# Gate and up projections of a decoder trunk as seven products of halves, two of their four weight sums added by transfers, and the down projection in three parts

## The chip, the core and the metric

One core of one Trainium2 chip runs the whole program. Engines are named as in the profile: PE (TensorE matmul), PEld (its weight load), DVE (VectorE), ACT (ScalarE), POOL (GpSimd), SP (SyncE, which here only issues transfers). The metric is the device time of one execution, in microseconds (us), from the first to the last instruction with the little that lies around them.

## The reference

Two decoder layers on x of 512 tokens by 1024 features, in float32. Each layer adds half a SwiGLU channel mixer, then a token mixer (block-sparse attention with a spatial gate in layer 0, differential attention in layer 1), then another half SwiGLU; a last RMS norm follows. There are so four channel mixers, and they hold most of the arithmetic:

```python
def swiglu(x, w_gate, w_up, w_down):          # w_gate, w_up: 1024 x 2816, w_down: 2816 x 1024
    return (jax.nn.silu(x @ w_gate) * (x @ w_up)) @ w_down
x = x + 0.5 * swiglu(rms_norm(x, ffn_pre_norm[layer]), ...)
```

## The kernel before

Features lie on the 128 partitions and tokens on the free axis, so x is 8 tiles of 128 x 512 (`x[k]`). A float32 matmul is made of three matmuls in the type fp32r: both operands are split into a high part (a copy to fp32r on ACT) and a low part (the difference, on DVE), and `mm3` (L151) adds high x high, high x low and low x high in PSUM. Weights come in raw chunks of 128 x 1024 words over SP's queue and are split in the same way: `split_to` (L83) makes `w_hi` on ACT (L89) and `w_lo` on DVE (L90).

A `Stream` (L62) holds the order of the work as slots. Each slot is a few products with the weight chunks that they take. `run` (L129) goes through the slots: it splits the chunks of this slot, issues the loads two chunks ahead, splits the next slot's chunks, traces the aftermath that earlier slots put off with `later`, and then the slot's products. Each engine takes its instructions in an order that the tile framework derives from this order of tracing and from what it reckons to be ready.

A channel mixer is `ffn` (L273). The 22 tiles of 128 of its hidden features are worked in two halves of 11. For each tile f there is a slot for gate and a slot for up: `project` (L266) runs 8 row tiles k with three matmuls of 512 columns each, 24 matmuls, into one PSUM bank. `product` (L277) then multiplies both banks by the norm's per-token factors (L279, L282), takes SiLU on ACT (L280), multiplies (L283) and splits the result (L262, L263). After 11 tiles `down` (L313) adds that half's part into each of the 8 output tiles: 11 x 3 matmuls of 512 columns per tile, in two chunks of 6 and 5 tiles, and then one DVE operation onto `x[d]` (L323). Behind the second half each finished `x[d]` is fed to the next norm: `Norm.split` (L196) makes the moving operands xh (ACT, L200) and xl (DVE, L201), and `square` (L204) adds up the squares, on POOL (L212, L214). The factors themselves come later (`only_row`, L230: two 512-column matmuls with ones and ten DVE operations).

A token mixer's last projection is `out_proj` (L340); it feeds the same norm. `Stream.begin` (L93) orders the loads and splits at the program's start.

## Time and profile before

| | |
|---|---|
| runs | 1917.41, 1915.25, 1915.66 us; median 1915.66 |
| profiled execution, first to last instruction | 1914.3 us (no other time of that execution is given) |
| instructions | 22078, of them 8692 matmuls |
| PE / DVE / ACT / POOL busy | 98% / 54% / 34% / 15% |
| DMA | 184 MB, 31% of the engines' time |
| HBM read | 174 MB, 92 GB/s |

How to read it: the span is the profiled execution's, and the median of the runs stands 1.4 us above it. A busy share is an average over stages. Matmuls overlap each other, so that a busy PE may still run below its pace: what tells is the distance from one start to the next.

### The profile page before, as it was taken

Reading aid. Unit: us, or ns where it says so; the run is one execution under the profiler, and the core shown is the slowest. Engines: PE = TensorE matmul, PEld = TensorE weight load, DVE = VectorE, ACT = ScalarE, POOL = GpSimd, SP = SyncE. Lnnn points to the kernel's source line nnn. Section 1 sums busy time; section 2 is a strip of 40 time slices with the busy share of each in tenths; the row PEclk is TensorE's granted clock in tenths of the full one; section 3 lists DMA queues with packets and bytes.
Section 4 is the critical chain, followed back from the end, with each engine's and each line's share of the span. In section 5 each row is a group of like instructions: output and inputs, shape, how many; then the busy total and the mean of one; then the engine's idle time right before and its main releaser. Section 6 shows DMA issues by size and latency. Waiting matters only on the chain.

```text
span 1914.3 us, 22078 instructions
## 1 busy us (share of the span) xinstructions
PE 1880.3 (98%) x8692; PEld 1568.1 (82%) x8692; DVE 1028.6 (54%) x1545; ACT 653.1 (34%) x993; POOL 283.8 (15%) x230
## 2 busy tenths in 40 slices
PE   8999999999999999999999999999899999999997
PEld 7888888888778888888888888888788788888886
DVE  7443444568766433444644344457788774434443
ACT  5222322334643222323332222234455432223221
POOL 0000001343440000002200000044333320000012
PEclk9999999999999999999999999999999999999998
DMA  5223332323213323333332332233233133233322
GB/s 182 99 80 107 99 99 84 125 88 100 89 56 99 99 84 105 98 92 91 106 98 84 102 110 97 79 114 110 89 89 89 36 119 98 79 110 99 99 84 82
DMA packets 58936, 184.31 MB, mean 96 GB/s; under 512 B 6848, under 2 KB 7504, under 8 KB 58832
## 3 DMA queue, kind: packets, MB, share of 16 engines
q1 hardware_dynamic: 58224, 181.82, 30.5%
q8 instruction: 68, 1.11, 0.2%
q10 hardware_dynamic: 576, 1.05, 0.1%
q14 instruction: 36, 0.29, 0.0%
q0 software_dynamic: 32, 0.03, 0.0%
HBM read 174.49 MB, written 2.10 MB: 92 GB/s over the span
## 4 chain that ended last, share of the span: by engine, by line
PE 87%; DVE 6%; POOL 3%; ACT 2%; issue 1%; DMA 0%; SPq 0%; DVEq 0%; POOLq 0%; ACTq 0%
PE py L152 10%; PE py L154 10%; PE py L153 10%; PE pu L154 8%; PE pu L152 8%; PE pu L153 8%; PE pg L153 8%; PE pg L154 8%; PE pg L152 8%; DVE w_lo L90 1%; POOL q L416 1%; PE pv L152 1%; PE pv L154 1%; PE pv L153 1%; PE pq L152 1%
## 5 line engine op out<-in xcount | busy, mean ns | idle before, releaser
L89 ACT ACTIVATE w_hi<-w_raw 128x1024 fp32r<-128x1024 f32 (+1 forms) x362 | 349.4, 966 | 958.5 <-PE py L153 323.8
L90 DVE TENSOR_TENSOR w_lo<-w_raw,w_hi 128x1024 fp32r<-128x1024 f32 (+1 forms) x362 | 414.2, 1144 | 201.9 <-ACT w_hi L89 201.3
L152 PE MATMUL pu<-xh,w_hi 128*128 128x512 f32 x736 | 286.7, 390 | 0.0
L154 PE MATMUL pu<-xh,w_lo 128*128 128x512 f32 x736 | 286.6, 389 | 0.0
L153 PE MATMUL pu<-xl,w_hi 128*128 128x512 f32 x736 | 286.6, 389 | 0.0
L152 PE MATMUL pg<-xh,w_hi 128*128 128x512 f32 x704 | 274.5, 390 | 5.1 <-ACT xh L200 5.1
L153 PE MATMUL pg<-xl,w_hi 128*128 128x512 f32 x704 | 274.6, 390 | 0.4 <-DVE xl L201 0.4
L154 PE MATMUL pg<-xh,w_lo 128*128 128x512 f32 x704 | 274.4, 390 | 0.0
L152 PE MATMUL py<-hh,w_hi 128*128 128x512 f32 x704 | 273.9, 389 | 0.0
L153 PE MATMUL py<-hl,w_hi 128*128 128x512 f32 x704 | 273.9, 389 | 0.0
L154 PE MATMUL py<-hh,w_lo 128*128 128x512 f32 x704 | 273.9, 389 | 0.0
L282 DVE TENSOR_TENSOR u<-pu,R 128x512 f32<-128x512 f32 x88 | 60.8, 691 | 267.0 <-PE pu L154 267.0
L212 POOL TENSOR_TENSOR acc<-x 128x512 f32<-128x512 f32 x6 | 9.2, 1539 | 1238.7 <-DVE x L323 1219.1
L153 PEld LDWEIGHTS pu<-xl,w_hi 128*128 128x128 f32 x736 | 138.4, 188 | 28.8
L154 PEld LDWEIGHTS pu<-xh,w_lo 128*128 128x128 f32 x736 | 138.3, 188 | 28.9
L152 PEld LDWEIGHTS pu<-xh,w_hi 128*128 128x128 f32 x736 | 138.4, 188 | 28.7
L152 PEld LDWEIGHTS pg<-xh,w_hi 128*128 128x128 f32 x704 | 132.4, 188 | 32.5 <-ACT xh L200 5.1
L153 PEld LDWEIGHTS pg<-xl,w_hi 128*128 128x128 f32 x704 | 132.4, 188 | 28.7 <-DVE xl L201 1.3
L154 PEld LDWEIGHTS pg<-xh,w_lo 128*128 128x128 f32 x704 | 132.4, 188 | 27.6
L153 PEld LDWEIGHTS py<-hl,w_hi 128*128 128x128 f32 x704 | 132.1, 188 | 27.5
L154 PEld LDWEIGHTS py<-hh,w_lo 128*128 128x128 f32 x704 | 132.1, 188 | 27.5
L152 PEld LDWEIGHTS py<-hh,w_hi 128*128 128x128 f32 x704 | 132.1, 188 | 27.3
(181 smaller groups left out, 2358.7 us busy)
## 6 DMA issues: line engine op xcount, KB each, us to landing
w_raw<-in_gu SPq DMA_DIRECT2D x174, 512.0 KB, 3.3
w_raw<-in_wd SPq DMA_DIRECT2D x64, 384.0 KB, 3.1
w_raw<-in_wd SPq DMA_DIRECT2D x64, 320.0 KB, 2.9
w_raw<-in_oqk SPq DMA_DIRECT2D x16, 512.0 KB, 3.3
ks<-ks SPq DMA_DIRECT2D x24, 256.0 KB, 3.5
w_raw<-in_eqk SPq DMA_DIRECT2D x8, 512.0 KB, 3.3
w_raw<-in_eo SPq DMA_DIRECT2D x8, 512.0 KB, 3.3
w_raw<-in_ov SPq DMA_DIRECT2D x8, 512.0 KB, 3.4
```

The lines of the kernel that those rows point to most:

```text
L89: nc.scalar.activation(hi, raw, AF.Copy)
L90: nc.vector.tensor_sub(lo, raw, hi.bitcast(F32))
L152: nc.tensor.matmul(o, sh, mh, start=first, stop=False)
L153: nc.tensor.matmul(o, sh, ml, start=False, stop=False)
L154: nc.tensor.matmul(o, sl, mh, start=False, stop=last)
L212: nc.gpsimd.tensor_mul(sq, x[k], x[k])
L282: nc.vector.tensor_mul(u, pu, norm.row)
L416: nc.gpsimd.tensor_add(q, q, sw)
```

## The change

The kernel works on pairs of hidden tiles, s and s + 11, and on gate and up of both at once. For a pair, the weights are a 2 x 2 block matrix (rows: tile s or s + 11; columns: the first or last 512 input features), a11, a12, a21, a22, each 128 x (gate, up) x 512 words. The moving side is a 2 x 2 block matrix too (first or last 512 features by first or last 256 tokens). A product of 2 x 2 blocks is made from seven block products, numbered 1 to 7 and run in the order 5, 6, 2, 7, 1 (of the next pair), 4, 3. Each is one slot of 4 row tiles x 2 (gate, up) x 3 matmuls of 256 columns, and three banks (A, B, D) collect them. Product 1 takes a11, 2 takes a12, 4 takes a22; 5 takes z = a21 + a22, 6 takes z + a11, 7 takes a21 + a11, and 3 takes a12 + (z + a11). In the first pair of each mixer all four sums are DVE additions of 1,024 words. In the others z and the operand of 7 are made by a plain load (SP) and a second load that adds onto it (`accum_op`, issued by POOL); the other two stay on DVE.

The aftermath of a pair: three ACT copies of bank A (v1, v2, v3), DVE additions and subtractions that make gate and up of both tiles from the copies and the banks, the multiplication by the factors, SiLU, the product and its split. The moving side needs seven split tiles per row tile instead of two half ones: `SevenNorm` makes them of x's halves, operands 1 and 5 when `x[0]` to `x[3]` come, the five others (`rest`) when `x[4]` to `x[7]` come. It replaces `Norm` for the four channel mixers; their factors are made as the token mixers' are (`sums`, `spread`), three slots later.

The down projection follows after pairs 0 to 3, 4 to 7 and 8 to 10. Its chunk per output tile holds both tiles of each pair, so that x gets three updates rather than two.

Slots of the channel mixers are `dense`: splits run four chunks ahead, sums one more, loads as far as six raw tiles allow. Raw chunks, halves and some mixer tiles share one pool of 14; scratch tiles go from 8 to 7 and the tiles that hold hidden features from 23 to 19.

```diff
-    BUFS = {"h": 23, "qk": 6, "tmp": 8, "row": 4}
+    BUFS = {"r2": 28, "h": 19, "tmp": 7, "row": 4}
...
+        return act.tile([P, 2, T], dt, name=name, tag="w4", bufs=14)
...
+                if dense:
+                    self.step()
+                    self.split_to(first + self.SPLIT)
+                    self.pre_to(first + self.SPLIT + 1)
+                    self.load(0, first + self.SPLIT + 8)
+                else:
+                    self.split_to(end)
+                    self.load(0, end + (2 if raws == 2 else 8))
...
+        def first(self, p):
+            self.halves(1, p, x[p][:, LO], self.gain(p))
+        def diff(self, p):
+            d = tmp("x1")[:, LO]
+            nc.vector.tensor_sub(d, x[p][:, LO], x[p][:, HI])
+            self.halves(5, p, d, self.gain(p))
+        def rest(self, p):
+            q = p + 4
+            g, n, nq = self.gain(q), neg_gains[:, self.idx, p:p + 1], neg_gains[:, self.idx, q:q + 1]
+            ta, tb = tmp("x37"), tmp("x64")
+            b22, x7, x6, x4 = ta[:, LO], ta[:, HI], tb[:, LO], tb[:, HI]
+            nc.scalar.activation(b22, x[q][:, HI], AF.Copy, scale=g)
+            nc.vector.scalar_tensor_tensor(x7, x[p][:, HI], n, b22, op0=OP.mult, op1=OP.add)
+            nc.vector.scalar_tensor_tensor(x6, x[p][:, LO], n, x7, op0=OP.mult, op1=OP.subtract)
+            self.halves(6, p, x6)
+            self.halves(2, p, x[q][:, LO], g)
+            nc.vector.scalar_tensor_tensor(x4, x[q][:, LO], nq, x6, op0=OP.mult, op1=OP.subtract)
+            self.halves(7, p, x7)
+            self.halves(4, p, x4)
+            self.halves(3, p, b22)
+        def feed(self, k):
+            if k < 4:
+                self.first(k)
+                self.diff(k)
+            else:
+                self.rest(k - 4)
+            self.square(k)
...
+    PARTS = ((0, 4), (4, 8), (8, HF))
+    ORDER = (5, 6, 2, 7, 1, 4, 3)
...
+                        if i == 0:
+                            nc.sync.dma_start(t, src)
+                        else:
+                            nc.gpsimd.dma_start(t, src, accum_op=OP.add)
...
+                if self.s > 0:
+                    by_sum = {
+                        5: lambda: Item([self.load("z", f1, 0, f1, 1)], raw("z"), frees=0),
+                        7: lambda: Item([self.load("c", f0, 0, f1, 0)], raw("c")),
+                        6: lambda: Item([], raw("z"), add("z", "z", "a11"), frees=0, free_pre=1),
+                        4: lambda: Item([self.load("a22", f1, 1)], raw("a22")),
+                    }
+                    if c in by_sum:
+                        return by_sum[c]()
+                return {
+                    1: lambda: Item([self.load("a11", f0, 0)], raw("a11"), frees=0),
+                    5: lambda: Item([self.load("a21", f1, 0), self.load("a22", f1, 1), new], raw("z"),
+                                    add("z", "a21", "a22"), frees=0),
+                    6: lambda: Item([], raw("z"), add("z", "z", "a11"), frees=0),
+                    2: lambda: Item([self.load("a12", f0, 1)], raw("a12"), frees=0),
+                    7: lambda: Item([], raw("a21"), add("a21", "a21", "a11"), free_pre=1),
+                    4: lambda: Item([], raw("a22")),
+                    3: lambda: Item([], raw("a12"), add("a12", "a12", "z"), free_pre=1),
+                }[c]()
...
+                    for p in range(4):
+                        t = norm.xt[c, p]
+                        for g in range(2):
+                            o = b[:, g * 256:(g + 1) * 256]
+                            s = slice((g * 4 + p) * P, (g * 4 + p + 1) * P)
+                            nc.tensor.matmul(o, w[0][:, s], t[:, 0], start=new and p + g == 0, stop=False, **go)
+                            nc.tensor.matmul(o, w[0][:, s], t[:, 1], start=False, stop=False, **go)
+                            nc.tensor.matmul(o, w[1][:, s], t[:, 0], start=False, stop=p == 3, **go)
...
+            def c11(self):
+                self.G = [self.both(), None]
+                nc.vector.tensor_add(self.G[0][:, :, LO], self.v_1, self.pair(self.bank["B"]))
+            def v3(self):
+                v = self.copied(-1.0)
+                self.G[1] = self.both()
+                g = self.G[1][:, :, HI]
+                nc.vector.tensor_sub(g, v, self.pair(self.bank["D"]))
+                nc.vector.tensor_mul(g, g, self.row(HI))
+            def c21(self):
+                nc.vector.scalar_tensor_tensor(self.G[1][:, :, LO], self.pair(self.bank["A"]), -1.0,
+                                               self.row(LO), op0=OP.mult, op1=OP.mult)
+                nc.scalar.activation(self.G[1][:, 0], self.G[1][:, 0], AF.Silu)
+            def c12(self):
+                g = self.G[0]
+                nc.vector.tensor_add(g[:, :, HI], self.v_2, self.pair(self.bank["D"]))
+                nc.vector.tensor_mul(g, g, self.row(slice(0, T)))
+                nc.scalar.activation(g[:, 0], g[:, 0], AF.Silu)
+            def h(self, n):
+                g = self.G[n]
+                nc.vector.tensor_mul(g[:, 1], g[:, 1], g[:, 0])
+                hi, lo = t2k("h", "hh", F32R), t2k("h", "hl", F32R)
+                nc.scalar.activation(hi, g[:, 1], AF.Copy)
+                H[self.s + n * HF] = (hi, lo)
+            def rest(self, n):
+                hi, lo = H[self.s + n * HF]
+                nc.vector.tensor_sub(lo, self.G[n][:, 1], hi.bitcast(F32))
...
+        for s0, s1 in PARTS:
+            for s in range(s0, s1):
+                for c in ORDER:
+                    if c != 1:
+                        add(s, c)
+                    elif s + 1 < HF:
+                        add(s + 1, 1)
+            cols = slice(s0 * P, s1 * P)
+            for ds in [(0, 1)] + [(d,) for d in range(2, KT)]:
+                st.add([chunk(wd[0, d][:, cols], wd[1, d][:, cols]) for d in ds], down(ds, s0, s1),
+                       dense=True, raws=6)
...
-    st.begin()
+    hi, lo = w4("w_hi", F32R), w4("w_lo", F32R)
+    for q, s in enumerate(cuts):
+        nc.scalar.activation(hi[:, :, s], a11[:, :, s], AF.Copy)
+        nc.vector.tensor_sub(lo[:, :, s], a11[:, :, s], hi[:, :, s].bitcast(F32))
+        for k in ((0,), (1,), (2, 3))[q]:
+            first.first(k)
+    st.pres = 1
+    st.halves.append([t.rearrange("p n t -> p (n t)") for t in (hi, lo)])
+    for k in range(4):
+        first.diff(k)
+    st.split_to(2)
+    for k in range(4):
+        first.rest(k)
+        if k == 1:
+            st.split_to(3)
+    for k in range(KT):
+        first.square(k, by_act=True)
     st.run()
```

## Rows read from the trace of the kernel before

**Rows 1.** The page: its span, part 1 (busy time, share of the span and instructions of each engine) and, of part 2, the granted TensorE clock in 40 slices, in tenths of full speed.

```profile
span 1914.3 us, 22078 instructions
...
PE 1880.3 (98%) x8692; PEld 1568.1 (82%) x8692; DVE 1028.6 (54%) x1545; ACT 653.1 (34%) x993; POOL 283.8 (15%) x230
...
PEclk9999999999999999999999999999999999999998
```

**Rows 2.** The page, part 4: the chain of work that ended last, its shares of the span by engine and by line.

```profile
PE 87%; DVE 6%; POOL 3%; ACT 2%; issue 1%; DMA 0%; SPq 0%; DVEq 0%; POOLq 0%; ACTq 0%
...
PE py L152 10%; PE py L154 10%; PE py L153 10%; PE pu L154 8%; PE pu L152 8%; PE pu L153 8%; PE pg L153 8%; PE pg L154 8%; PE pg L152 8%; DVE w_lo L90 1%; POOL q L416 1%; PE pv L152 1%; PE pv L154 1%; PE pv L153 1%; PE pq L152 1%
```

**Rows 3.** PE's waits over the whole span: who waited for whom, us in total, times, longest.

```profile
PE py L154 <- DVE w_lo L90: 5.3, 2, 3.1
...
PE pg L152 <- ACT xh L200: 5.1, 1, 5.1
...
PE pr L240 <- DVE lcol L184: 2.0, 1, 2.0
```

**Rows 4.** Busy time (and instructions) of each engine in four stretches: us from the span's start, length, then PE, PEld, DVE, ACT, POOL, the granted clock, the DMA engines' share and GB/s.

```profile
0.00:20.00 20.00, 14.49 (x52) 11.12 (x53) 14.07 (x26) 15.39 (x26) 2.13 (x9) 1.00 0.75 251
...
20.00:366.00 346.00, 346.00 (x1528) 286.52 (x1527) 165.13 (x197) 101.35 (x126) 21.66 (x13) 1.00 0.31 99
...
550.00:570.00 20.00, 17.76 (x78) 14.24 (x78) 19.12 (x17) 8.04 (x10) 17.57 (x11) 1.00 0.17 55
...
1520.00:1540.00 20.00, 16.90 (x74) 13.47 (x74) 19.13 (x18) 8.55 (x11) 17.63 (x12) 1.00 0.16 53
```

**Rows 5.** Timeline of a gate projection: start us, duration us, engine, line, operation. One split of a 1,024-word chunk on VectorE with GpSimd idle; the first of 24 matmuls of 512 columns, and the first of the next 24.

```profile
58.88 1.22 DVE L90 TENSOR_TENSOR w_lo<-w_raw,w_hi 128x1024 fp32r<-128x1024 f32 x1 [0.23 <-ACT w_hi L89]
...
63.21 0.39 PE L152 MATMUL pg<-xh,w_hi 128*128 128x512 f32 x1
...
68.65 0.39 PE L152 MATMUL pu<-xh,w_hi 128*128 128x512 f32 x1
```

**Rows 6.** Timeline of PE in the odd mixer's values, the first of 96 matmuls of 256 columns and the first matmul behind them; and that matmul's weight load among the groups by line and form (busy us, mean ns of one).

```profile
1312.77 0.28 PE L152 MATMUL pv<-w_hi,xh 128*128 128x256 f32 x1
...
1324.28 0.28 PE L456 MATMUL s<-ks,qs 128*128 128x256 f32 x1
...
L152 PEld LDWEIGHTS pv<-w_hi,xh 128*128 128x128 f32 x192 | 36.6, 190 | 2.6
```

**Rows 7.** The two steps of a row of factors on PE: a piece of the chain in order of time (start us, us, what), and the timeline of the end.

```profile
373.45 0.79 PE pc L223 x8
...
1904.31 1.12 PE L240 MATMUL pr<-ident,lcol 128*128 128x128 f32 x4 [2.04 <-DVE lcol L184]
```

**Rows 8.** Groups of instructions by line and form over the whole span: out<-in, tile, count, busy us, mean ns of one, idle before it.

```profile
L90 DVE TENSOR_TENSOR w_lo<-w_raw,w_hi 128x1024 fp32r<-128x1024 f32 x234 | 300.1, 1283 | 74.6 <-ACT w_hi L89 74.5
...
L89 ACT ACTIVATE w_hi<-w_raw 128x1024 fp32r<-128x1024 f32 x234 | 247.7, 1060 | 617.2 <-PE pg L153 241.3 <-issue 234.2 <-PE py L153 63.6
...
L279 DVE TENSOR_TENSOR g<-pg,R 128x512 f32<-128x512 f32 x88 | 60.8, 691 | 170.8 <-PE pg L154 170.7
...
L280 ACT ACTIVATE g<-g 128x512 f32<-128x512 f32 x88 | 54.2, 616 | 16.0 <-DVE g L279 16.0
...
L323 DVE SCALAR_TENSOR_TENSOR x<-py,x 128x512 f32<-128x512 f32 x64 | 44.3, 692 | 127.7 <-PE py L154 127.7
...
L90 DVE TENSOR_TENSOR w_lo<-w_raw,w_hi 128x768 fp32r<-128x768 f32 x64 | 61.4, 959 | 0.7 <-ACT w_hi L89 0.3
...
L201 DVE SCALAR_TENSOR_TENSOR xl<-x,gains,xh 128x512 fp32r<-128x512 f32 x48 | 64.4, 1355 | 3.3 <-ACT xh L200 3.2
```

**Rows 9.** The page, part 6: DMA issues, count, KB each, median us from issue to landing.

```profile
w_raw<-in_gu SPq DMA_DIRECT2D x174, 512.0 KB, 3.3
```

**Rows 10.** Timeline of the start.

```profile
1.33 0.71 POOL L162 DMA_DIRECT2D gains<-in_gains  x1 [0.81 <-POOLq L923]
...
3.60 0.43 DVE L108 TENSOR_TENSOR w_lo<-w_raw,w_hi 128x256 fp32r<-128x256 f32 x1 [2.36 <-ACT w_hi L107]
...
4.99 0.40 ACT L107 ACTIVATE w_hi<-w_raw 128x256 fp32r<-128x256 f32 x1
...
5.12 0.75 DVE L201 SCALAR_TENSOR_TENSOR xl<-x,gains,xh 128x512 fp32r<-128x512 f32 x1 [1.10 <-ACT xh L200]
...
5.14 0.79 PE L152 MATMUL pg<-xh,w_hi 128*128 128x512 f32 x1 [5.14 <-ACT xh L200]
...
8.59 0.68 DVE L214 TENSOR_TENSOR acc<-acc,sq 128x512 f32<-128x512 f32 x1
```

**Rows 11.** Busy time by engine (columns as in rows 4) across the first slots of the second channel mixer.

```profile
568.00:578.00 10.00, 10.00 (x46) 8.29 (x45) 9.06 (x8) 3.87 (x6) 6.06 (x4) 1.00 0.46 147
...
578.00:588.00 10.00, 10.00 (x46) 8.28 (x45) 6.08 (x10) 2.67 (x3) 0.00 (x0) 1.00 0.34 106
```

**Rows 12.** Timeline of VectorE and of GpSimd while a channel mixer's last outputs come.

```profile
901.94 1.53 DVE L201 SCALAR_TENSOR_TENSOR xl<-x,gains,xh 128x512 fp32r<-128x512 f32 x1
...
901.20 1.73 POOL L212 TENSOR_TENSOR sq<-x 128x512 f32<-128x512 f32 x1 [4.06 <-DVE x L323]
```

More of the change, by code (lines that the diff above doesn't have):

```diff
@@ L149, in trunk_kernel, with chunk, load @@
     st = Stream()
+    def chunk(*srcs):
+        keep = {}
+        def load():
+            t = w4("w_raw").rearrange("p n t -> p (n t)")
+            o = 0
+            for s in srcs:
+                nc.sync.dma_start(t[:, o:o + s.shape[1]], s)
+                o += s.shape[1]
+            keep["raw"] = t[:, :o]
+        return Item([load], lambda: keep["raw"])
     def mm3(o, sh, sl, mh, ml, first, last):
@@ L275, in ffn @@
         H = {}
-        def product(f, pg, pu):
-            g = tmp("g")
-            nc.vector.tensor_mul(g, pg, norm.row)
-            nc.scalar.activation(g, g, AF.Silu)
-            u = tmp("u")
-            nc.vector.tensor_mul(u, pu, norm.row)
-            nc.vector.tensor_mul(u, u, g)
-            H[f] = split(u, "h", "h")
-        def first(wg, wu):
-            wait = int(which == 0)
-            st.later(1 + wait, norm.only_row)
-            pg, pu = bank("pg"), bank("pu")
-            for ks in [[k] for k in range(KT)] if which == 0 else (range(KT - 1), range(KT - 1, KT)):
-                for b, w in ((pg, wg), (pu, wu)):
-                    project(b, w, norm, ks)
-            st.later(2 + wait, lambda: product(0, pg, pu))
@@ new lines, in ffn, with add, begin @@
+        steps = [Step(s, any(s == e - 1 for _, e in PARTS)) for s in range(HF)]
+        def add(s, c):
+            st.add([steps[s].item(c)], steps[s].slot(c), dense=True, raws=6)
+        add(0, 1)
+        first, end, fn, dense, raws = st.slots[-1]
+        def begin(w):
+            norm.finish_soon(3)
+            fn(w)
+        begin.tiles = steps[0].raw
+        st.slots[-1] = (first, end, begin, dense, raws)
+        for s0, s1 in PARTS:
[9 more added lines that the diff above has]
+                       dense=True, raws=6)
```

338 lines of the change are left out of this document (197 added, 141 removed).

## The prediction, made before the change was run

> **What bounds the kernel now.** I read the page first: PE is busy for 98% of the span and at the upper clock (2.4 GHz granted, 10 tenths of it) except at the very end [rows 1]. Busy PE is not proof, because matmul ends are modelled, so I read the chain of waits next: 87% of it is PE, nearly all in the gate, up and down products [rows 2]. Then PE's own list of waits: no long wait repeats, the largest is 5.3 us in two pieces at a mixer's end [rows 3]. Then the windows: through a channel mixer PE idles 0.00 us of 346 while VectorE is busy 165 us, ScalarE 101 us and the DMA engines 31% [rows 4]. So in the channel mixers (about 1,436 of 1,914 us) only PE's own pitch counts. The timeline gives it: 24 matmuls of 512 columns take 68.65 - 63.21 = 5.44 us, 0.2267 us each [rows 5].
>
> **The products.** I count by the pair of 128-wide feature tiles f and f+11; there are 44 pairs in four channel mixers. Before, a pair takes 4 projections x 24 = 96 matmuls of 512 columns: 96 x 0.2267 = 21.76 us. After, seven products x 4 row tiles x 2 (gate, up) x 3 = 168 matmuls of 256 columns. The question is whether a 256-column matmul hides its weight load. The odd mixer's values have that very shape, three matmuls with a fresh 128x128 load each: 96 of them in 1324.28 - 1312.77 = 11.51 us, 0.1199 us each, while a load shows 0.190 us and lies beside the matmul before it [rows 6]. So a pair takes 168 x 0.1199 = 20.14 us, one product 2.88 us. Saved: 44 x 1.62 = **71.1 us**; not the eighth that the count promises (2.72 per pair), because the part that does not shrink with the columns, 2 x 0.1199 - 0.2267 = 13 ns per matmul, is paid 1.75 times as often.
>
> **The row of factors.** Column sums and four transposes replace two 512-column matmuls: 0.79 + 1.12 [rows 7] - 0.45 = +1.5 us, four times; the second piece ran at the end, where the clock had fallen to 0.8, so I take **+4** (0 to 6).
>
> **Projection down in three parts.** 528 matmuls per channel mixer stay. Eight more updates of x, 0.69 us each on VectorE [rows 8], lie beside 5.44 us of PE per output tile: nothing. Without that cover they would be 5.5 us each mixer.
>
> **VectorE inside a pair.** Before: 4 splits x 1.22 [rows 5] (1.28 is the mean over the span, with GpSimd at times beside it [rows 8]) + 8 x 0.69 [rows 8] = 10.4 us of 21.76. After: 7 splits (8.5), 2 sums of 1,024 words at the price of a split (2.4), and the recombination, nine 512-wide operations and one of 1,024 (7.4): **18.4 us of 20.14**. ScalarE: 7 x 1.06 + 7 x 0.62 = 11.8 us [rows 8]. So PE still sets the pace, with 1.7 us to spare; VectorE can run near that, as it is busy 19.12 of 20 us at a mixer's end [rows 4]. Three slots of splits stand ready, and each slot's recombination comes before its split, so a delay of a slot reaches no matmul. The first pair makes all four sums on VectorE: 20.9 us, 0.8 over, in three channel mixers (the first one counts below): **+2.4** (0 to 5).
>
> **Transfers.** Two of the four weight sums of a pair move to transfers: one half is loaded by SP, the other is added by a transfer that POOL issues. Chunks per pair go from 4 to 7, 3.67 MB in 20.14 us, 182 GB/s; 99 GB/s took 31% [rows 4], so 182 take 57% by share: hidden. An adding transfer waits for the plain one (3.3 us to landing [rows 9]); behind that wait on POOL stand only the next such transfer and, in the last third, the norm's squares. The sum is split five to seven slots later, 14 to 20 us: hidden. An issue on POOL cost 0.71 us, for 28 KB in 128 rows [rows 10]; the price of one that adds 512 KB in 256 rows is not in the trace. Bounds: two a pair at 0.71 fit into VectorE's spare 1.7 even if all of it came off VectorE, which is nothing; two at twice that, 2.8, do not. I take nothing, by the row as it stands; the upper end is a rival.
>
> **The start.** VectorE must make, before the fourth product can begin: the low parts of the first chunk (1.55), four first tiles (4 x 0.43 [rows 10]), four differences (8 x 0.43), the second product's sum and split (2.44), `rest` four times (32 x 0.43 = 13.8), the third's sum and split (2.44) and the fourth's split (1.22): 26.6 us. It begins at 3.60 and so ends at 30.2; by then PE has three products, 8.6 us, and is 21.6 late. Before, 52 matmuls (11.8 us) stand in the first 20 [rows 4]: 8.2 late. **+13**; +6 if the last four operations of each `rest` are put off, +18 if the seven sums of squares (4.8 [rows 10]) come first.
>
> **From a mixer to a channel mixer, twice.** VectorE's norm tiles cost 8 x 0.75 = 6.0 before and 12 x 0.43 + 32 x 0.43 = 18.9 after; two weight sums come on top: 15.3 more. VectorE is full there already (19.12 and 19.13 of 20 us, with PE idle 2.2 and 3.1 [rows 4]) and has 0.9 + 3.9 = 4.9 us free in the following 20 [rows 11]. That leaves 10.4, of which some of the last `rest` can wait: **+9 each, 18** (3 to 15 each).
>
> **From channel mixer to channel mixer, once.** The last third gives 8 x 4.08 = 32.6 us of PE. VectorE: 8 x (0.69 + 0.96 [rows 8]) + 18.9 = 32.1, and 7.3 for the first four products; cover 32.6 + 8.6 = 41.2. Alone this fits, with 1.8 to spare. But GpSimd squares there, and beside it the normalizing operation took 1.53 us [rows 12] (1.36 on the mean of 48 [rows 8]) in place of 0.75 [rows 10]. Sixteen such meetings would cost 16 x 0.78 = 12.5, 10.7 over the spare; none would cost nothing. I take **+5** (0 to 11), since the update of x reads PSUM and some meetings fall on it. The Trainium skill, SBUF — State Buffer, section "SBUF: two separate sides", lets VectorE's operations with two SBUF inputs and GpSimd's hold a shared port in turn, for whole instructions; taken strictly that puts the term at its upper end. The trace agrees in kind: the operation doubles.
>
> The mixers' buffers change (scratch tiles from 8 to 7, 23 to 19, chunks and keys in one pool): nothing, up to 5 either way out of the 34.0 us that PE is not busy in the whole span [rows 1].
>
> **Sum.** 1914.3 - 71.1 + 4 + 13 + 18 + 5 + 2.4 = 1885.6. The profiled execution has its span alone; the median of the runs is 1.4 above it. Forecast **1887 us**, 1.5% faster; with the terms at their ends 1857 to 1915.
>
> **Rivals.**
> (a) The seams are covered: splits and sums are made early where VectorE waits, and only the start and some of the mixers' ends stay. For: VectorE is idle for 181 of 346 us of a channel mixer before [rows 4]. Against: at the seams it is full. 1914.3 - 71.1 + 4 + 6 + 6 + 1.4 = 1861, down to 1850 if the mixers gain; I count what ends below 1866 to this case.
> (b) Slower: VectorE becomes the bound of every pair, because POOL's work for an adding transfer blocks it. Price: two issues of 1.42 us, 18.4 + 2.8 = 21.3 us a pair, 1.2 over PE; 40 pairs, +48: 1935. It decides from 1.7 + 28.7 / 40 = 2.4 us a pair. For: the doubled operation of [rows 12]. Against: there GpSimd computed on SBUF, and the one issue seen is 0.71 us.
> (c) The adding transfers are the bound, by their rate or because POOL gets them out late. Plain, 512 KB take 0.524 / 319 GB/s = 1.64 us of all engines; the room is 20.14 - 11.5 = 8.6 us a pair, so an adding one may cost 3.6 times that. At four times it is 21.3 us a pair and again about 1934. For: it reads its target too. Against: reading once more makes two, not four. The same page and section of the Trainium skill warns that a transfer issued by GpSimd starves while VectorE runs in a mode that takes both ports; no run here shows it.
> That the change does not do what it says: a product might have to wait for a bank that ScalarE has yet to copy (the second product on bank A follows one slot later); ScalarE's 59% makes that small, and I put it within the forecast.
>
> **Chances.** Forecast's case 0.62 (0.04 of it within 0.2%), (a) 0.18, (b) 0.13, (c) 0.07. About 0.2%, 3.8 us, is what a measurement of this kernel can tell from no change: faster 0.62 - 0.04 + 0.18 = 0.76, same 0.04, slower 0.20. The range takes in (a) but for its last end and (b) and (c) to their prices above: 1852 to 1931 leaves out some 0.04 below and 0.14 above.
>
> **What would show it.** Right: matmuls of 256 columns 0.120 us apart; PE without gaps inside the thirds; VectorE above 85% there; gaps of some 20 us in the first 40 and near 10 behind each mixer; DMA share near 55%. Wrong: a pitch above 0.125, PE waiting for low halves pair after pair (b), for a chunk on a transfer (c), or for ScalarE's copies; or seams without gaps (a).

## The result, and the profile after

The changed kernel takes **1942.97 us** (median; 1942.32 to 1946.13), the kernel before, on the same chip, 1915.55 (1915.25 to 1917.41): ratio 1.0144, 95% interval 1.0129 to 1.0159. It is 1.4% slower; the forecast was 1.5% faster.

The page of the kernel after, answering [rows 1] and [rows 2]: busy time and share of each engine, the granted clock in 40 slices, the chain's shares, and two rows of its DMA issues [rows 9].

```profile
span 1941.2 us, 29617 instructions
...
PE 1834.8 (95%) x11900; PEld 1681.6 (87%) x11900; DVE 1413.3 (73%) x1999; ACT 882.4 (45%) x1319; POOL 365.3 (19%) x310
...
PEclk7999999999997999999999999999999979999999
...
PE 80%; DVE 11%; POOL 4%; ACT 3%; issue 2%; DMA 1%; SPq 0%; DVEq 0%; POOLq 0%; ACTq 0%
...
w_raw<-in_gu SPq DMA_DIRECT2D x215, 512.0 KB, 4.4
w_raw<-in_gu POOLq DMA_DIRECT2D x80, 512.0 KB, 7.2
```

PE is busy 45.5 us less, but its idle time goes from 34.0 to 106.4 us. The reader is to see that PE's share fell and that the clock fell in three slices (the start and behind each token mixer), where it had been at the top before. Where the idle time sits is told by two views. First PE's waits (who for whom, us in total, times, longest), answering [rows 3]:

```profile
PE pA L406 <- ACT v L418: 16.2, 2, 15.4
PE pD L406 <- ACT w_hi L120: 15.9, 3, 7.4
PE py L170 <- DVE w_lo L121: 15.3, 2, 8.2
PE pc L240 <- POOL acc L231: 11.3, 1, 11.3
PE pA L406 <- ACT w_hi L1056: 9.9, 1, 9.9
PE pD L408 <- DVE w_lo L121: 7.4, 4, 3.4
...
```

Few waits, each long: nothing repeats pair after pair. Then the windows by stage (length, then PE, PEld, DVE, ACT, POOL, granted clock, DMA share, GB/s). The stages are channel mixer, token mixer, two channel mixers, token mixer, channel mixer; each begins with its first matmul. After:

```profile
0.00:376.10 376.10, 348.89 (x2388) 326.81 (x2389) 273.40 (x335) 174.95 (x233) 47.91 (x42) 0.97 0.57 154
376.10:598.00 221.90, 203.82 (x965) 168.52 (x964) 151.46 (x281) 96.73 (x192) 83.39 (x78) 0.96 0.24 74
598.00:953.90 355.90, 346.91 (x2389) 325.32 (x2389) 260.75 (x303) 161.29 (x206) 42.04 (x32) 0.98 0.55 143
953.90:1315.40 361.50, 346.04 (x2390) 324.18 (x2389) 265.57 (x310) 163.70 (x211) 53.79 (x38) 0.98 0.55 145
1315.40:1570.90 255.50, 239.34 (x1365) 209.13 (x1365) 208.54 (x466) 125.34 (x278) 93.17 (x88) 0.97 0.26 79
1570.90:1926.80 355.90, 346.88 (x2389) 325.30 (x2388) 246.20 (x289) 159.74 (x202) 44.99 (x36) 0.98 0.51 135
```

Before, the same stages:

```profile
0.00:367.80 367.80, 362.29 (x1586) 299.13 (x1587) 179.99 (x222) 116.74 (x152) 23.79 (x22) 1.00 0.34 107
367.80:570.20 202.40, 197.10 (x964) 164.57 (x964) 143.01 (x263) 95.56 (x181) 86.38 (x76) 0.99 0.28 87
570.20:929.90 359.70, 359.70 (x1589) 297.84 (x1588) 172.31 (x202) 106.22 (x132) 25.68 (x16) 1.00 0.32 98
929.90:1289.60 359.70, 359.70 (x1589) 297.84 (x1588) 168.57 (x199) 104.24 (x130) 23.46 (x14) 1.00 0.31 97
1289.60:1540.10 250.50, 238.90 (x1365) 208.37 (x1364) 200.08 (x449) 126.12 (x268) 100.03 (x87) 0.99 0.28 85
1540.10:1899.60 359.50, 359.50 (x1587) 297.77 (x1586) 157.24 (x192) 103.54 (x130) 24.43 (x16) 1.00 0.31 94
```

Within a channel mixer all is as forecast. The first matmuls of two products on the timeline of PE, and a window of 20 us:

```profile
60.09 0.28 PE L406 MATMUL pA<-xt,w_hi 128*128 128x256 f32 x1
...
62.97 0.28 PE L406 MATMUL pB<-xt,w_hi 128*128 128x256 f32 x1
```

```profile
180.00:200.00 20.00, 20.00 (x169) 20.00 (x169) 16.95 (x20) 11.28 (x14) 2.38 (x2) 1.00 0.74 185
```

2.88 us a product, PE without a gap, VectorE at 85%, 185 GB/s. Most of the loss is at the **seams**, where one stage's last blocks of x become the next one's tiles (the start and part of the first token mixer come below). There VectorE has no gap: before, between two channel mixers, PE did not idle at all; after, from 955 to 975 us, VectorE is busy 20.00 of 20 and PE 5.29.

```profile
955.00:975.00 20.00, 5.29 (x42) 4.88 (x40) 20.00 (x34) 11.48 (x25) 8.43 (x6) 0.77 0.17 52
```

What stretches VectorE's work there is seen when its timeline (first fence) is laid beside GpSimd's (second), start and duration in us:

```profile
944.08 1.26 DVE L268 SCALAR_TENSOR_TENSOR xt<-x,gains,xt 128x256 fp32r<-128x256 f32 x1
945.27 1.50 DVE L277 TENSOR_TENSOR x<-x 128x256 f32<-128x256 f32 x1
947.35 0.48 DVE L268 SCALAR_TENSOR_TENSOR xt<-x,gains,xt 128x256 fp32r<-128x256 f32 x1 [0.58 <-ACT xt L267]
...
951.81 2.31 DVE L362 TENSOR_TENSOR w_raw<-w_raw 128x1024 f32<-128x1024 f32 x1
```

```profile
943.44 1.62 POOL L229 TENSOR_TENSOR sq<-x 128x512 f32<-128x512 f32 x1 [2.09 <-DVE x L485]
945.14 1.35 POOL L231 TENSOR_TENSOR acc<-acc,sq 128x512 f32<-128x512 f32 x1
...
951.68 1.35 POOL L231 TENSOR_TENSOR acc<-acc,sq 128x512 f32<-128x512 f32 x1
```

The same operation takes 0.48 us alone and 1.26 when it starts inside a GpSimd square; the subtraction that starts at 945.27 ends at 946.77, 0.28 after GpSimd's add; the weight sum that starts 0.13 us after an add takes 1.10 us longer than alone (1.21). In these rows whichever starts second ends after the first.

Counted over the timelines of the whole seam (905 to 985 us), each of its 14 GpSimd operations stretches one VectorE operation that starts while it runs. That one ends 0.28 us after the GpSimd operation when it has 256 columns, 1.08 or 1.09 us after it when it has 1,024. Its time less the median of its form in run 1 below, summed over the 14, is **12.9 us**; at the other two seams it is 12.0 us each. None of them is an update of x: no update starts while one of these runs, and those that do in runs 7 and 8 below keep their 0.68 us.

### The profile page after: what moved, and what is told of

Read it like the earlier page. It is cut to its first block, busy times and chain, and to the rows that moved or that the text cites. A ratio compares the mean times of both kernels' runs of the same rounds, so it can differ in the third digit from the quotient of the medians.

```text
span 1941.2 us, 29617 instructions
## 1 busy us (share of the span) xinstructions
PE 1834.8 (95%) x11900; PEld 1681.6 (87%) x11900; DVE 1413.3 (73%) x1999; ACT 882.4 (45%) x1319; POOL 365.3 (19%) x310
## 4 chain that ended last, share of the span: by engine, by line
PE 80%; DVE 11%; POOL 4%; ACT 3%; issue 2%; DMA 1%; SPq 0%; DVEq 0%; POOLq 0%; ACTq 0%
PE pA L406 9%; PE py L168 9%; PE py L169 9%; PE pA L407 9%; PE pA L408 9%; PE py L170 8%; PE pD L408 4%; PE pD L407 4%; PE pD L406 4%; PE pB L406 2%; PE pB L407 2%; PE pB L408 2%; DVE w_lo L121 2%; DVE xt L268 1%; POOL q L592 1%
## 5 line engine op out<-in xcount | busy, mean ns | idle before, releaser
L120 ACT ACTIVATE w_hi<-w_raw 128x1024 fp32r<-128x1024 f32 (+1 forms) x455 | 473.7, 1043 | 614.8 <-PE py L169 228.1
L121 DVE TENSOR_TENSOR w_lo<-w_raw,w_hi 128x1024 fp32r<-128x1024 f32 (+1 forms) x455 | 565.1, 1242 | 183.5 <-ACT w_hi L120 151.2
L406 PE MATMUL pA<-xt,w_hi 128*128 128x256 f32 x1408 | 401.5, 285 | 26.1 <-ACT v L418 16.2
L407 PE MATMUL pA<-xt,w_hi 128*128 128x256 f32 x1408 | 400.2, 284 | 0.0
L408 PE MATMUL pA<-xt,w_lo 128*128 128x256 f32 x1408 | 399.9, 284 | 0.0
L406 PEld LDWEIGHTS pA<-xt,w_hi 128*128 128x128 f32 x1408 | 272.4, 193 | 28.0 <-ACT v L418 18.0
L407 PEld LDWEIGHTS pA<-xt,w_hi 128*128 128x128 f32 x1408 | 272.3, 193 | 0.1
L408 PEld LDWEIGHTS pA<-xt,w_lo 128*128 128x128 f32 x1408 | 271.9, 193 | 0.2 <-DVE w_lo L1057 0.2
L406 PE MATMUL pD<-xt,w_hi 128*128 128x256 f32 x704 | 202.4, 287 | 15.9 <-ACT w_hi L120 15.9
L408 PE MATMUL pD<-xt,w_lo 128*128 128x256 f32 x704 | 202.6, 288 | 7.4 <-DVE w_lo L121 7.4
L407 PE MATMUL pD<-xt,w_hi 128*128 128x256 f32 x704 | 201.9, 287 | 0.0
L406 PEld LDWEIGHTS pD<-xt,w_hi 128*128 128x128 f32 x704 | 137.9, 196 | 16.8 <-ACT w_hi L120 16.5
L408 PEld LDWEIGHTS pD<-xt,w_lo 128*128 128x128 f32 x704 | 137.9, 196 | 8.0 <-DVE w_lo L121 8.0
L407 PEld LDWEIGHTS pD<-xt,w_hi 128*128 128x128 f32 x704 | 138.0, 196 | 0.3
```

The lines of the kernel that those rows point to most:

```text
L120: nc.scalar.activation(hi, raw, AF.Copy)
L121: nc.vector.tensor_sub(lo, raw, hi.bitcast(F32))
L406: nc.tensor.matmul(o, w[0][:, s], t[:, 0], start=new and p + g == 0, stop=False, **go)
L407: nc.tensor.matmul(o, w[0][:, s], t[:, 1], start=False, stop=False, **go)
L408: nc.tensor.matmul(o, w[1][:, s], t[:, 0], start=False, stop=p == 3, **go)
```

## The experiments

Every ratio is to the kernel before, with its 95% interval; "after" is 1942.97. An edit is against the changed kernel unless it says otherwise. Stage lengths in us, from the first matmul of a stage to that of the next:

```
                          channel1 token1 channel2 channel3 token2 channel4   total
before                       367.8  202.4    359.7    359.7  250.5    359.5  1915.6
forecast                     364.0  202.4    352.7    348.7  250.5    352.5  1887
after                        376.1  221.9    355.9    361.5  255.5    355.9  1943.0
seam squares left out        375.8  214.2    350.5    345.0  250.0    350.5  1902.2
rest pieces left out         364.1  221.7    345.3    353.7  256.5    344.6  1903.0
both left out                364.9  212.7    343.4    343.2  248.0    343.5  1875.1
best version                 378.4  210.0    354.1    346.2  245.2    354.9  1904.8
```

**1. GpSimd's squares left out at the three seams** (13 of 14 GpSimd operations of each, and ScalarE's one square).

```diff
-            self.square(k)
+            if k == 0:
+                self.square(k)
```

> Leaves out seven of the eight squares, with their additions, that GpSimd makes for the norms of the second, third and fourth channel mixer (so their factors are not the reference's); nothing else changes. Theory S (VectorE's own queue of moving tiles, sums and splits at the seams is what PE waits for): GpSimd's share is small, 5 to 10 us off 1943, about 1935; PE's waits at the seams stay above 45 us. Rival L (GpSimd holds VectorE up there, the doubled operations): 25 to 35 us off, 1908 to 1918, and the mean of the 256-wide operations on x falls from 0.79 us to the 0.48 seen alone.

Measured 1902.18 us, 0.9926 (0.9911 to 0.9941): 41 us gone, more than any expectation. VectorE's operations are back at their own length; groups by line and form (count, busy us, mean ns) after, and then without the squares:

```profile
L268 DVE SCALAR_TENSOR_TENSOR xt<-x,gains,xt 128x256 fp32r<-128x256 f32 x48 | 37.4, 794 | 3.4 <-ACT xt L267 3.4
...
L277 DVE TENSOR_TENSOR x<-x 128x256 f32<-128x256 f32 x16 | 15.0, 953 | 0.0
```

```profile
L268 DVE SCALAR_TENSOR_TENSOR xt<-x,gains,xt 128x256 fp32r<-128x256 f32 x48 | 23.8, 511 | 3.9 <-ACT xt L267 3.9
...
L277 DVE TENSOR_TENSOR x<-x 128x256 f32<-128x256 f32 x16 | 6.4, 417 | 0.0
```

**2. Three of four row blocks without their `rest` tiles** (the first block's are used).

```diff
+            if p > 0:
+                for c in (6, 2, 7, 4, 3):
+                    self.xt[c, p] = self.xt[c, 0]
+                return
```

> Leaves out the five later moving tiles for three of the four row tiles of each channel mixer (the first one's are used in their place): 24 VectorE and 18 ScalarE operations less per seam and at the start; matmuls stay. Theory S: 3 x 3.4 = 10 us per seam, four times, plus some of the half clock behind the gaps: 40 to 60 us off 1943, so 1885 to 1903, faster than the kernel before; PE's long waits at the seams fall below 4 us each. Rival L: 10 to 20 us off, since the squares still meet the splits and sums. Rival M (the mixers' shared buffers are the main loss): under 15 us off.

Measured 1902.95, 0.9934 (0.9919 to 0.9949): 40 us gone with all squares in place: by the stages 12 at the start, where there are no GpSimd squares, and 29 at the seams. Here less work on VectorE (and on ScalarE, which loses 18 operations a seam) does what undisturbed work did in run 1.

**3. Dummy matmuls in the gaps**, so that PE's clock stays up: in front of the first pair's third product at the start or second behind a token mixer, in the third channel mixer's sums, and in the output projection.

```diff
+    def fill(n, t):
+        b = bank("fill")
+        for i in range(n):
+            nc.tensor.matmul(b, t[:, :P], t, start=i == 0, stop=i == n - 1)
...
```

> Adds matmuls of 512 columns into a spare bank where PE waits: 55 before the first mixer's third product, 27 before the second product of the second and fourth mixer, 40 before the third mixer's sums, 24 before the third chunk of each token mixer's last projection; nothing depends on them. Theory C (the half clock behind the gaps costs by itself: PE is busy 1834.8 us where 1880.3 - 71.1 + 4 = 1813 was due, so some 20 us): the granted clock stays at the upper level in the gaps, and 8 to 18 us come off 1943. If the clock is not the cost: no change, or up to 5 us more where the added matmuls outlast a wait.

Measured 1947.52, 1.0161 (1.0146 to 1.0176); mean granted clock 0.986 for 0.973. The clock is up in part (before, 0.995) and no time is won, as it would be if PE, done sooner, only waited longer for VectorE and ScalarE. That is not shown by this run alone: where the dummies outlast a gap they cost time themselves (the third channel mixer takes 366.0 us for 361.5).

**4. The start in another order**: `rest` tiles and squares issued three and four products later.

```diff
-    for k in range(4):
-        first.rest(k)
-        if k == 1:
-            st.split_to(3)
-    for k in range(KT):
-        first.square(k, by_act=True)
+    st.later(3, lambda: [first.rest(k) for k in range(4)])
+    st.later(4, lambda: [first.square(k, by_act=True) for k in range(KT)])
```

> At the start alone: the five later moving tiles and the squares are traced behind the first copy of bank A and the second product, not ahead of them. Theory A (PE's 15.4 us wait there is for a copy that stands behind 20 us of tile work in ScalarE's queue): 8 to 14 us off 1943, 1929 to 1935, and no wait of PE for a copy of bank A over 3 us. Rival (the start is bound by VectorE's total, whatever the order): under 3 us off.

Measured 1942.65, 1.014 (1.0123 to 1.0157). The wait of 15.4 us for ScalarE's copy is gone and others stand in its place (2.5 us for the copy, 8.1 for tiles); the first stage ends at 376.0 as ever. So the releaser that the profile names was only the last of several; that all of them stand behind VectorE's list, which is full from 20 to 40 us, is the reading that fits.

**5. Runs 1 and 2 together.**

> Leaves out seven of the eight GpSimd squares and adds of a seam (three seams) and the rest pieces of three of four row blocks (the pieces of the first block are used in their place). Theory Q (one queue: VectorE's work of a seam, each 256-wide operation stretched by GpSimd's squares, overruns what the products cover; taking either away ends most of the overrun): the two together save little more than either, since each alone saves about 40 us; from the shortest of each stage in the two single runs (364.1 + 214.2 + 345.3 + 345.0 + 250.0 + 344.4 + 14.4) 1872 to 1884 us. Rival A (two separate losses that add): 1943 - 41 - 40 = 1862, 1857 to 1867 us.

Measured 1875.11, 0.9779 (0.9765 to 0.9794), in the range of the one queue and above that of two losses that add. The stages say more than the sum. In the third channel mixer, behind the second, the runs take off 16.5 and 7.8 us singly and 18.3 together, not 24.3: there the loss is used up. Behind the token mixers (token mixer and channel mixer together) it is 13.1 and 10.8 singly, 21.7 together, and 10.9 and 10.3, 19.9 together: nearly the sum, as it would be where VectorE's list is too long by more than either. Both fit one list that counts only by what stands over. With the seams nearly empty a channel mixer takes 343.2 to 343.5 us, 16.0 to 16.5 less than before; the forecast for products, row of factors and first sums alone is -17.8 + 1 + 0.8 = -16.0.

**6. Squares by ScalarE, adds by VectorE**, the last four blocks' behind the seam, nothing left out.

```diff
-            self.xt = {}
+            self.xt, self.behind = {}, []
...
-            self.square(k)
+            if k < 4:
+                self.square(k, by_act=True)
+            else:
+                self.behind.append(k)
+
+        def finish_soon(self, wait=1):
+            for i, k in enumerate(self.behind):
+                st.later(1 + i, lambda k=k: self.square(k, by_act=True))
+            super().finish_soon(wait + int(len(self.behind) > 0))
```

> Nothing left out: the squares of the channel mixers' norms go from GpSimd to ScalarE and their adds to VectorE, those of the last four row blocks in the first four products of the next channel mixer, and the sums one product later. Theory Q: VectorE's operations of the seam go back from 950 to about 420 ns, and its adds of 0.69 us come on top, three in the seam and four behind it: 1900 to 1917 us. Rival W (the work of the squares itself, wherever it is done, is what the seam can't hold, since VectorE has 100% there): 1925 to 1943 us.

Measured 1914.53, 0.9988 (0.9978 to 0.9997): 28 us below after, although VectorE got 7 adds of 0.69 us more per seam, three in it and four behind it. What hurt was not the amount of the squares' work but which engine did it and when; run 7 changes the engine alone.

**7. Squares by ScalarE, adds still by GpSimd** (first diff): 21 GpSimd operations in the three seams. **8. Squares twice by GpSimd** (second): 63. After has 42, run 1 has 3 (the expectations below take it for none).

```diff
+        def square(self, k, by_act=False):
...
+            nc.scalar.activation(sq, x[k], AF.Square)
+            if not new:
+                (nc.vector if by_act else nc.gpsimd).tensor_add(self.acc, self.acc, sq)
```

```diff
+            if k < KT - 1:
+                nc.gpsimd.tensor_mul(tmp("sq"), x[k], x[k])
             self.square(k)
```

> Nothing left out: in the channel mixers' norms the squares go to ScalarE, their adds stay on GpSimd; so 21 of the 42 GpSimd operations of the three seams go. Theory H (each GpSimd operation with two operands from SBUF holds VectorE up once, by some 0.8 to 1 us; removing all 42 gave 41 us): half of it, 1919 to 1926 us. Rival C (the loss comes from GpSimd's chain ending late, after which the sums of squares wait): GpSimd's chain is halved, but VectorE's operations stay as slow: 1930 to 1943 us, with the mean of the 256-wide subtraction still above 0.9 us.

> Adds work: GpSimd makes seven of a seam's eight squares twice, 21 operations more at the three seams. Theory H: 21 x 0.8 to 1 us more, 1958 to 1966 us, and the mean of VectorE's 256-wide operations rises again. Rival C (only the end of GpSimd's chain matters, which is late at one of the three seams): 10 us or less more, 1945 to 1953 us.

Measured 1923.34, 1.0033 (1.0023 to 1.0043), and 1958.89, 1.0211 (1.0196 to 1.0226). By the number of GpSimd operations, 3, 21, 42, 63: 1902.2, 1923.3, 1943.0, 1958.9 us. That is (1923.3 - 1902.2) / 18 = 1.2, then 0.9, then 0.8 us per operation. The subtraction, which stands where the squares are, goes with them; first run 7, then run 8:

```profile
L277 DVE TENSOR_TENSOR x<-x 128x256 f32<-128x256 f32 x16 | 6.2, 416 | 0.0
```

```profile
L277 DVE TENSOR_TENSOR x<-x 128x256 f32<-128x256 f32 x16 | 16.9, 1075 | 0.0
```

What the GpSimd operations stretch VectorE by, added up over the three seams from the timelines as for after, goes the same way: 17.2 us in run 7, 36.9 in after, 50.7 in run 8, where the times stand 21.2, 40.8 and 56.7 us above run 1.

The rival, that the late end of GpSimd's own chain is what counts, falls for the whole: in run 7 PE still waits 8.5 us for GpSimd's last add (11.3 in after) and the time is 20 us shorter. At the seam before the third channel mixer, where that wait lies, it keeps a part that no run separates: run 1 leaves the wait out together with the squares, and takes off 16.5 us there for 12.9 of stretching.

**9. Blocks of x in the order 0, 4, 1, 5, 2, 6, 3, 7** in the last down products and the output projections, so that `rest` is not bunched behind block 4.

```diff
-            for ds in [(0, 1)] + [(d,) for d in range(2, KT)]:
+            for ds in [(0, 4)] + [(d,) for d in (1, 5, 2, 6, 3, 7)]:
...
-            done_ks = {d: [] for d in range(4)}
+            early = (0, 4, 1, 5)
+            done_ks = {d: [] for d in early}
...
```

> Nothing left out or added: only the order of the eight row blocks of x in the last down products and in the output projections changes, 0, 4, 1, 5, 2, 6, 3, 7 instead of 0 to 7, so that the halves that need two blocks are made two blocks apart instead of all behind block 4. Theory Q in the form that the backlog comes from bunching (some 20 us of 256-wide work and 5.5 us of updates fit into the eight blocks' 43 us, but not into the last four's 22): most of what the single removals gave comes back at the seams between channel mixers, less behind the mixers: 1890 to 1912 us. Rival W (what counts is the sum of VectorE's work, stretched by the squares, wherever it stands): 1930 to 1943 us.

Measured 1940.76, 1.0127 (1.0112 to 1.0142). My form of the theory falls: it is not the bunching but the sum. The channel mixers win what the token mixers in front of them lose (second stage 226.2, fifth 260.8).

**10. All four weight sums by VectorE in every pair**, no adding transfer.

```diff
-                if self.s > 0:
+                if False:
                     by_sum = {
```

> Nothing left out: all four sums of weights by VectorE in every pair, none by an adding transfer. VectorE is 85% busy in a pair of 20.16 us and gets 2 x 1.22 us more: 19.5 of 20.16 us. Theory S (the pair still fits, and the adding transfers bought nothing in the stages between the seams): 1940 to 1950 us. Rival V (at 97% VectorE delivers some halves late, a microsecond or two in each of 40 pairs, and no longer works off the seam's backlog): 1960 to 2020 us.

Measured 1944.54, 1.0138 (1.0123 to 1.0154): the same as after. The window that answers to the one above:

```profile
180.00:200.00 20.00, 20.00 (x169) 20.00 (x168) 19.06 (x22) 10.70 (x15) 0.00 (x0) 1.00 0.33 106
```

VectorE at 95%, PE still without a gap: in the stages' middles the transfers cost nothing and buy nothing.

**11. The first pair of every later channel mixer too with adding transfers** (`if self.s > 0 or which > 0`).

> Nothing left out: in the second to fourth channel mixer the first pair too takes two of its four sums by adding transfers. Theory Q: 2 x 1.22 us of VectorE's work leave each of three seams in which VectorE is the bound: 7 us at least, more where they were stretched: 1928 to 1937 us. Rival T (the adding transfers come late at a seam, where GpSimd's queue holds squares ahead of their issue): the wait for VectorE turns into one for the transfers, 1943 to 1955 us.

Measured 1938.59, 1.0114 (1.0097 to 1.0131), 4 us below after, at the edge of the intervals and less than the 7 expected: not settled. It speaks against transfers that come late, which would have made it longer.

**12. The start without seven of its eight squares.** **13. The kernel before with seven scratch tiles.**

```diff
-    for k in range(KT):
-        first.square(k, by_act=True)
+    first.square(0, by_act=True)
```

```diff
-    BUFS = {"h": 23, "qk": 6, "tmp": 8, "row": 4}
+    BUFS = {"h": 23, "qk": 6, "tmp": 7, "row": 4}
```

> Leaves out seven of the eight squares and their adds of the first norm alone, at the start (4.8 us of VectorE, 4.4 of ScalarE). Theory V (the start ends when VectorE's list ends, so the adds that stand in it are 5 of the 12 us by which the start was forecast too short): the first channel mixer ends at 369 to 372 us instead of 376, the whole 1936 to 1940. Rival L (the start is bound by loads and by the weights' sums, the adds run beside): no change, 1941 to 1945.

> The kernel before with seven scratch tiles instead of eight, as the changed kernel has, and nothing else. Theory T (the missing scratch tile is the part of the first mixer's loss, about 10 us, that stays when the seams are empty): that mixer goes from 202.4 to 207 to 212 us and the second one up as well: 1921 to 1930 us. Rival N (the scratch tile costs nothing, as was forecast for it): 1914 to 1918 us.

Measured 1935.75, 1.0100 (1.0083 to 1.0117), with the first stage ending at 368.0 for 376.1; and 1916.10, 1.0000 (0.9991 to 1.0010). The squares and their adds do hold up the start, by more than the adds' 4.8 us on VectorE; as 4.4 us of ScalarE's squares go with them, the share of each engine is not separated. The scratch tile costs nothing.

**14. The first token mixer's gate tiles from another pool**, and **15. a third loaded chunk in the token mixers.**

```diff
-            gv = [two("gv") for _ in range(2)]
             for t in range(TT):
-                g = gv[t // 2][:, t % 2]
+                g = t2k("r2", "gv")
```

```diff
-        def add(self, items, fn, dense=False, raws=2):
+        def add(self, items, fn, dense=False, raws=3):
```

> Nothing left out: the four gate tiles of the first token mixer are taken from the pool of 2 KB tiles instead of the weights' pool of fourteen 4 KB tiles. Theory P (the first mixer's gap of some 7 us at 420 to 435 us is weights that wait for tiles that the gate holds): that mixer goes from 221.9 to 213 to 217 us, the whole to 1934 to 1939. Rival G (the gate's own work on VectorE and GpSimd holds the splits up, whoever owns the tile): no change, 1941 to 1945.

> Nothing left out: in the token mixers three loaded weight tiles may wait for their split instead of two. Theory P (the first mixer's waits for weight halves, 5.2 us at its value product, are loads asked for too late, now that they share one pool with everything else): that mixer goes from 221.9 to 214 to 218 us, the whole to 1935 to 1940. Rival G (VectorE stands at its gate's operations, and the splits behind them): no change, 1940 to 1946 us.

Measured 1945.71, 1.0150 (1.0135 to 1.0165), and 1944.05, 1.0146 (1.0131 to 1.0161): neither helps. With the third chunk the first token mixer gains 2.8 us and the second loses 3.3; but runs 4 and 12, which leave that mixer as it is, shorten it by 2 us as well.

**16. Versions that beat both.** Run 9's order with run 6's squares; and that with adding transfers in every first pair.

> Nothing left out: the blocks in the order 0, 4, 1, 5, 2, 6, 3, 7, and the squares off GpSimd (ScalarE squares, VectorE adds, the last four behind the seam). Theory Q: both loosen the same queue, so the two together reach what the removal of squares and rest pieces together left, plus the start's 11 us that stays: 1878 to 1895 us. Rival W: the adds that VectorE gets cost what the missing squares give: 1900 to 1920 us.

> As the run before (pairs of blocks, squares off GpSimd), and the first pair of every channel mixer too takes two of its sums by adding transfers. Theory Q: at the start, where VectorE is the bound for 30 us, 2.4 us less; nothing more at the other seams, where VectorE is no longer late: 0 to 5 us below the run before. Rival T (adding transfers come late at a seam): up to 10 us above it.

Measured 1909.76, 0.9967 (0.9955 to 0.9980), and **1904.79, 0.9937 (0.9923 to 0.9952)**. The first did not reach the 1878 to 1895 expected of it and lies in the rival's 1900 to 1920, by which VectorE's adds cost part of what the squares gave: behind the token mixers VectorE is still nearly full (18.91 of 20 us from 580 to 600 in the last version), and the channel mixers there take 354.1 and 354.9 us for 343.4 and 343.5 with both left out. The second's 5 us were expected at the start, but its first stage is 2 us longer; they came later. The last version, nothing left out, is 0.6% faster than the kernel before: 13.5 us less in the third channel mixer (346.2 for 359.7), 10.6 more in the first stage. Its page:

```profile
PE 1831.0 (96%) x11900; PEld 1675.9 (88%) x11900; DVE 1379.2 (72%) x2012; ACT 888.8 (47%) x1340; POOL 313.9 (16%) x276
...
PEclk7999999999999999999999999999999999999998
```

## Why the prediction was wrong

By stage, forecast against measured change: first channel mixer -3.8 against +8.3, first token mixer 0 against +19.5, second channel mixer -7.0 against -3.8, third -11.0 against +1.8, second token mixer 0 against +5.0, fourth channel mixer -7.0 against -3.6. The misses sum to 56 us, none of them in the middle of a channel mixer.

- **The products, 71.1: right.** 2.88 us a product, and 16.0 to 16.5 us a channel mixer with the row and the first sums once the seams are nearly empty (run 5; forecast 16.0).
- **VectorE inside a pair, and the transfers at nothing: right.** 16.95 of 20 us where 18.4 of 20.14 was reckoned (18.3 of 20). An issue on POOL took 1.19 us, not 0.71, and landing 7.2; two of those did not make VectorE late. So rivals (b) and (c) fall, although the time lies where they had put it: right size, wrong mechanism. Run 10 takes the adding transfers away and gives the same time.
- **From channel mixer to channel mixer, +5 (0 to 11): the step that failed first.** "Alone this fits, with 1.8 to spare" is nearly borne out: without the squares the stage takes 345.0, 1.3 more than the forecast without this term. The meetings with GpSimd were put at sixteen of 0.78 [rows 12], 12.5 us, and then at half of what stood over, on the ground that some fall on the update of x. What failed is that discount: all 14 meetings fall on other operations, 12.9 us in the trace, and run 1 took 16.5 us off this stage (the last add's wait, above, goes with it). The stretching goes straight into the time where VectorE has no slack. The Trainium skill, SBUF — State Buffer, section "SBUF: two separate sides", makes the shared port "an **exclusive lock**, not a bandwidth split", held for a whole instruction. The timeline at 945 us agrees with it to a tenth or two of a microsecond. Taken strictly it would have given the upper end, 11, and even that was too low for the stage.
- **From a mixer to a channel mixer, 9 each: same fault, larger.** The sum there priced `rest` at its undisturbed 0.43 us, with no term for GpSimd at all, though the same squares run there. Leaving them out gives 7.7 + 5.4 us at the first (token mixer and channel mixer) and 5.5 + 5.4 at the second. What is left of the two terms is then 8.3 us, without the mixer's own 10.3 of the next point, and 6.5: near the 9 that VectorE's list alone was given.
- **The mixers' buffers, nothing: wrong for the first token mixer by some 10 us.** Of its +19.5, 9.2 go with the seam (run 5). The rest stays: not the gate's tiles (14) or the scratch tile (13), and the number of loaded chunks (15) for 3 us at most. The trace shows where it is. Two chunks of value weights had landed at 378.9 and 408.3 us, but their copies stand in ScalarE's list behind copies of the gate (`gh`), which wait for GpSimd; ScalarE's timeline after:

```profile
419.79 0.63 ACT L317 ACTIVATE gh<-gv 128x512 fp32r<-128x512 f32 x1 [7.08 <-POOL gv L794]
420.33 1.04 ACT L120 ACTIVATE w_hi<-w_raw 128x1024 fp32r<-128x1024 f32 x1
...
430.04 0.63 ACT L317 ACTIVATE gh<-gv 128x512 fp32r<-128x512 f32 x1 [2.77 <-POOL gv L794]
430.57 1.99 ACT L120 ACTIVATE w_hi<-w_raw 128x1024 fp32r<-128x1024 f32 x2
```

  Before, the same two copies ran ahead of the first `gh`:

```profile
401.93 1.06 ACT L89 ACTIVATE w_hi<-w_raw 128x1024 fp32r<-128x1024 f32 x1 [3.90 <-PE pu L153]
...
407.37 1.06 ACT L89 ACTIVATE w_hi<-w_raw 128x1024 fp32r<-128x1024 f32 x1 [2.15 <-PE pu L153]
411.87 0.63 ACT L262 ACTIVATE gh<-gv 128x512 fp32r<-128x512 f32 x1 [3.44 <-POOL gv L613]
```

  So PE waits 5.2 us for these halves and then runs at the lower clock (0.83 granted from 430 to 440 us), and the value product ends 77.8 us into the stage for 69.9; another 2 us go to a longer wait later in the mixer (`ml`, 2.4 us for 0.4). Why the copies come in that order, and whether the shared pool has to do with it, is open. Run 15 bears the reading out in part: there the second copy starts 4.7 us earlier in the stage, and the value product ends 3.5 us earlier.
- **The start, +13: short by 12.** VectorE's list was to end at 30.2 us, and 18 was named for the case that the seven sums of squares come first. They do, ahead of the fourth product; VectorE is full from 20 to 40 us (windows below, columns as above), and leaving them out gives 8 back (run 12). The first matmul started at 9.9 us for 5.14 [rows 10], which had no term either.

```profile
20.00:30.00 10.00, 1.38 (x11) 1.18 (x9) 10.00 (x22) 7.21 (x18) 1.22 (x1) 0.67 0.52 106
30.00:40.00 10.00, 3.19 (x15) 3.19 (x16) 9.79 (x19) 8.10 (x17) 0.00 (x0) 0.50 0.00 0
```

- **The clock had no term.** PE's busy time fell by 45.5 and not by 67.1 us, because of matmuls at the lower level, 1.2 GHz, beside the gaps (granted clock 0.50 from 30 to 40 us, above; by the clock's records PE is busy at that level for 49.7 us, 11.0 before). Run 3 speaks against this as a loss of its own, though not with certainty: with part of the clock held up the time did not fall.
- **The sum and the readings, redone.** The sum holds. Its ends, 1857 and 1915, leave out the 5 us either way that the buffers were given. PE's largest single wait before was not in the two pieces at a mixer's end: it was one of 5.4 us in a token mixer; nothing rests on that.

So the mechanism that was named for one seam, and priced there at half, decided at three: the squares on GpSimd cost 41 us (run 1) where the forecast had 5, and that is 36 of the 56 us missed. The start has 12, 8 of them with its squares (run 12), the first token mixer's own 10, and the smaller terms take back 2.

## What to carry to other kernels

When a change moves work onto an engine at a stage's edge, sum that engine's list there with the durations it has beside its neighbours, not alone, and look at what else runs in the same 20 us. Give each instruction of a neighbour that is seen to stretch the engine's operations one meeting, undiscounted. Whatever shortens such a list gives time back, so move the part that another engine can do, here the squares to ScalarE, which was busy for 45% of the span.

## What the hardware showed that was not expected

At these seams, where VectorE is full, a GpSimd operation on 128x512 words costs more than half of its own time: 1.2, 0.9 and 0.8 us of the kernel's time each (runs 7 and 8), for mean durations of 1.4 to 1.6 us. The meetings are regular: all 42 of after stretch one VectorE operation each, by 0.34 to 1.10 us, and a 256-column one ends 0.28 us after GpSimd's, while updates of x, which read one operand in PSUM, keep their 0.68 where they start while a GpSimd operation runs (runs 7 and 8). An adding transfer of 512 KB takes 7.2 us to land for 4.4 of a plain one, and GpSimd 1.19 us to issue. With VectorE busy 19.06 of 20 us, PE still ran without a gap.
